# Layer 0 and the SSD norms re-cut: row sums in column groups, seven conv taps on VectorE, shift dots on TensorE, shift reads on SyncE's queue

## The chip, the cores and the metric

One core of a Trainium2 chip runs the whole kernel. The metric is the device time of one execution in microseconds (us), smaller is better. The kernel before took 1365.77 us in the median of 3 runs (1363.56 to 1369.64).

## The reference: what is computed

A trunk of two layers over x of 512 tokens by 1024 features in float32. Each layer is a mixer and a ConvFFN, each behind an RMSNorm that a condition vector c scales and shifts. The change touches layer 0's norm and mixer (a combined projection that feeds sliding-window attention and a Conformer convolution of 31 taps with a LayerNorm) and, in layer 1's Mamba-2 mixer, the `dt` projection and the four grouped norms.

```python
mod = silu(c) @ w_mod[i] + b_mod[i]
sh_m, sc_m, g_m, sh_f, sc_f, g_f = split(mod, 6)
h = rmsnorm(x, norm_mix[i]) * (1.0 + sc_m) + sh_m
...
def even_mixer(h, ...):
    q, k, v, conf_in = split(h @ w_in + b_in)
    merged = concat([swa_sink_attention(q, k, v, ...), conformer_conv(conf_in, ...)])
    return merged @ w_out

def conformer_conv(u, conv_w, conv_b, ln_g, ln_b):
    a, g = split(u, 2)
    h = causal_dwconv(a * sigmoid(g), conv_w, conv_b)      # 31 taps, 512 channels
    mu, var = mean(h), mean(square(h - mu))                # over the 512 channels
    return silu((h - mu) * rsqrt(var + LN_EPS) * ln_g + ln_b)
...
y = yg * rsqrt(mean(yg * yg, axis=-1) + NORM_EPS)          # ssd_mixer, 4 groups of 512 features
```

## The kernel before

**Layout.** Activations lie with 128 features on the partitions and 512 tokens in the free dimension. A weight is split in two rounded parts (`wh`, `wl`), an activation likewise (`hn` holds such pairs), and one product of 128 by 128 weights is three matmuls of 512 columns (`mm3`, lines 365 to 367). A product of 128 output features over 1024 inputs is thus 24 matmuls. Weights come in tiles `raw` of 512 KB on SyncE's (SP's) queue (line 304), ScalarE (ACT) rounds them to `wh` (line 312) and VectorE (DVE) makes `wl` (line 317).

**Order of the work.** Each mixer is a list of tasks with an engine, a cost, predecessors, and buffers taken and given back. `Plan.run` simulates the engines with those costs and, whenever one is free, emits its ready task of highest rank: the length of the path behind it plus a weight for its label from a table of numbers (`MIXER0`, `MIXER1`). Each engine and each DMA queue then runs its instructions in the order in which they were emitted.

**Layer 0's norm.** x comes in 8 tiles; ACT squares each (line 672); line 679 sums a square over its features with four matmuls of one column (the square is the weight, ones the moving column), 32 matmuls in all; ACT takes the root (699); `rstd_newton` (lines 405 to 409) refines it on DVE in five small instructions of 4 columns; `spread` (line 399) turns the columns into a row on all partitions. Then per feature tile: DVE computes the scale and the shift of the condition as a dot of 1024 columns each (`mod_dot`, line 571), `normed`, `upper` and `lower` (741, 745, 749) make the pair `hn`, and the first six outputs of the projection accumulate as `hn` appears (line 753). Line 651 issues idle matmuls (fillers) at three places of the norm.

**Convolution.** 512 channels are four chunks. A chunk's gated input (line 869) is stored to DRAM (872) and read back by `conv_fetch` (886) as four tiles `s`, one per 32 channels, each holding four shifted copies of these channels; stores and reads are issued on GpSimd's (POOL's) queue. `conv_product` (893) adds the taps in steps: a step is four matmuls of 512 columns, one for each group of 32 output channels, which covers four taps; eight steps (`CQ`) make 31 taps. Weights of these matmuls are diagonal blocks built by DVE (877); ACT adds the bias (898). The LayerNorm's mean is four matmuls with ones (1119), its squares' sums are 16 one-column matmuls (1110), then root, `rstd_newton` and `spread` as above.

**Layer 1.** `dt_in` is 24 matmuls with weights of 32 columns, `dt_tokens` four transposes; each of the four scan groups ends with the sums of `sz` (line 391, 4 matmuls), a root (1607), `rstd_newton` and `spread` before its rows can enter the output product.

Of the kernel before, what the change touches and what calls it, by code (L numbers as in the profile page):

```python
# [16 lines left out]
F32 = mybir.dt.float32  # L17
# [7 lines left out]
P = 128  # L25
# [9 lines left out]
CTAPS, CQ = 4, 8  # L35
# [4 lines left out]
_VEC = [("bmod", 96), ("nmix", 16), ("nffn", 16), ("fnorm", 8), ("bin", 14), ("ccw", 128), ("eye", 32),  # L40
# [29 lines left out]
WARM = (2, 2, 3)  # L70
# [152 lines left out]
def trunk(ctx: ExitStack, tc: tile.TileContext, xT_d, vecs_d, rows_d, dsk_d, pos_d, const_d, wss_d, wg0_d,  # L223
# [178 lines left out]

    def rstd_newton(ss, sd, width, e=0, n=NCH):
        v, y, a, y2 = (small(n) for _ in range(4))
# [216 lines left out]
    def even_layer(lp, cp, dp0):  # L621
# [26 lines left out]
        def warm(n):  # L648

            for _ in range(n):  # L650
                mm(g0[NG0 - 1][:, 0:2 * P], lhsT=ident, rhs=con[:, :2 * P], start=True, stop=True)
# [58 lines left out]
        rb_ = add("x_row", "PE", 2.1, x_row, [t], dict(ps=1))  # L710
# [54 lines left out]
        for kt in range(KT):  # L765
# [8 lines left out]
            s_ = add("h_dot", "DVE", 1.3, lambda kt=kt: mod_dot(st["ss", kt, 1], modv[:, 0, kt:kt + 1]), [ss_, *cbs], None, dict(mr=1))  # L774
            s_ = add("h_bias", "ACT", 0.29, lambda kt=kt: shift(kt), [s_, vl_])
# [1112 lines left out]
```

## Time and profile before

| what | value |
|---|---|
| median of 3 runs | 1365.77 us |
| profiled execution, time of its own | 1364.35 us |
| its span in the trace | 1362.5 us |
| mean granted TensorE clock | 0.986 |
| TensorE (PE) busy | 1335.4 us, 98% |
| VectorE (DVE) busy | 852.4 us, 63% |
| ScalarE (ACT) busy | 590.5 us, 43% |

The span is the time from the first to the last instruction that the profiler recorded; 1.85 us of the execution lie outside of it. Durations and sums below come from this one execution. [...]

### The profile page before, as it was taken

To read this page: it belongs to the slowest core of one execution; us is meant where nothing else is said; L and a number is where in the kernel's file an instruction comes from. 1 tells how busy PE (TensorE), PEld (TensorE's weight loads), DVE (VectorE), ACT (ScalarE), POOL (GpSimd) and SP (SyncE) were. 2 spreads that over 40 slices of the span, in tenths; PEclk is the share of its full clock that TensorE was granted. 3 is DMA by queue.
4 is the path that set the end of the run, shared out by engine and by line. 5 is a ranking of instruction groups with operands and counts; after the bars stand their busy time and mean duration, and the time that the engine had idled before them with its cause. 6 is when DMAs were issued, how large, how long until landed. Compare 5 with 4: busy or idle time off the path is not lost.

```text
span 1362.5 us, 17553 instructions
## 1 busy us (share of the span) xinstructions
PE 1335.4 (98%) x6878; PEld 1093.9 (80%) x6879; DVE 852.4 (63%) x1316; ACT 590.5 (43%) x938; POOL 95.7 (7%) x173
## 2 busy tenths in 40 slices
PE   8979999999999999999999999999999999999997
PEld 7726778988888888898887887878898888888886
DVE  5912898786576567667588684788665434444443
ACT  4512763543233223246686762765354313322333
POOL 5420110000000000010010100110000000000001
PEclk7989999999999999999999999999999999999998
DMA  9595453475565565322552432432223233223311
GB/s 333 194 191 129 138 194 118 140 232 172 183 210 168 183 214 191 105 89 67 153 169 79 156 93 80 139 126 79 76 78 111 90 100 107 92 89 108 100 55 63
DMA packets 58212, 183.71 MB, mean 135 GB/s; under 512 B 10064, under 2 KB 13200, under 8 KB 58128
## 3 DMA queue, kind: packets, MB, share of 16 engines
q1 hardware_dynamic: 45184, 152.24, 35.2%
q0 software_dynamic: 12256, 29.69, 7.5%
q8 instruction: 54, 0.88, 0.3%
q10 hardware_dynamic: 688, 0.66, 0.2%
q14 instruction: 30, 0.25, 0.1%
HBM read 179.26 MB, written 3.28 MB: 134 GB/s over the span
## 4 chain that ended last, share of the span: by engine, by line
PE 87%; DMA 4%; DVE 3%; issue 2%; ACT 2%; POOL 1%; DVEq 0%; ACTq 0%; POOLq 0%
PE ps L365 26%; PE ps L367 26%; PE ps L366 26%; DMA s<-uc 2%; PE ps L893 2%; DMA M<-scr 2%; PE ps L399 1%; PE ps L391 1%; PE ps L1573 1%; PE ps L679 1%; ACT M L1523 1%; PE ps L1565 1%; PE ps L1551 1%; DVE mr L571 1%; PE ps L1041 0%
## 5 line engine op out<-in xcount | busy, mean ns | idle before, releaser
L365 PE MATMUL ps<-hn,wh 128*128 128x512 f32 (+1 forms) x1214 | 460.1, 379 | 0.8 <-ACT hn L441 0.8
L366 PE MATMUL ps<-hn,wh 128*128 128x512 f32 (+1 forms) x1214 | 454.1, 374 | 0.4
L367 PE MATMUL ps<-hn,wl 128*128 128x512 f32 (+1 forms) x1214 | 454.0, 374 | 0.0
L317 DVE TENSOR_TENSOR wl<-raw,wh 128x1024 fp32r<-128x1024 f32 (+1 forms) x208 | 250.8, 1209 | 144.4 <-ACT wh L312 143.4
L312 ACT CAST wh<-raw 128x1024 fp32r<-128x1024 f32 (+1 forms) x208 | 213.1, 1028 | 219.2 <-PE ps L366 209.9
L365 PEld LDWEIGHTS ps<-hn,wh 128*128 128x128 f32 x1214 | 228.6, 188 | 43.0 <-issue 1.7
L366 PEld LDWEIGHTS ps<-hn,wh 128*128 128x128 f32 x1214 | 228.7, 188 | 42.0 <-issue 1.4
L367 PEld LDWEIGHTS ps<-hn,wl 128*128 128x128 f32 x1214 | 228.5, 188 | 41.0
L454 DVE SCALAR_TENSOR_TENSOR x<-ps,modv,x 128x512 f32<-128x512 f32 (+1 forms) x108 | 73.7, 689 | 119.6 <-PE ps L367 119.4
L365 PE MATMUL ps<-fh,wh 128*128 128x512 f32 (+1 forms) x380 | 142.2, 374 | 0.0
L366 PE MATMUL ps<-fl,wh 128*128 128x512 f32 (+1 forms) x380 | 141.9, 373 | 0.0
L367 PE MATMUL ps<-fh,wl 128*128 128x512 f32 (+1 forms) x380 | 141.9, 373 | 0.0
L571 DVE SCALAR_TENSOR_TENSOR mr<-mr,cb 128x1024 f32<-128x1024 f32 x96 | 116.1, 1218 | 3.5 <-DMA mr<-in_wss_dram 2.2
L1281 ACT ACTIVATE tmp<-ps,vecs 128x512 f32<-128x512 f32 x44 | 34.3, 780 | 115.4 <-PE ps L367 115.4
L1282 DVE SCALAR_TENSOR_TENSOR tmp<-ps,vecs,tmp 128x511 f32<-128x511 f32 x44 | 32.9, 748 | 80.0 <-ACT tmp L1281 80.0
L366 PEld LDWEIGHTS ps<-fl,wh 128*128 128x128 f32 x380 | 71.5, 188 | 12.8
L365 PEld LDWEIGHTS ps<-fh,wh 128*128 128x128 f32 x380 | 71.5, 188 | 12.6
L367 PEld LDWEIGHTS ps<-fh,wl 128*128 128x128 f32 x380 | 71.5, 188 | 12.6
L429 POOL TENSOR_TENSOR ssq<-ssq,tmp 128x512 f32<-128x512 f32 x10 | 13.4, 1338 | 805.1 <-ACT tmp L428 805.1
L290 ACT CAST fh<-tmp 128x512 fp32r<-128x512 f32 x44 | 27.3, 620 | 96.4 <-DVE tmp L1286 96.4
L1284 ACT ACTIVATE tmp<-tmp 128x512 f32<-128x512 f32 x44 | 27.8, 633 | 74.9 <-DVE tmp L1283 74.9
L291 DVE TENSOR_TENSOR fl<-tmp,fh 128x512 fp32r<-128x512 f32 x44 | 30.5, 693 | 30.2 <-ACT fh L290 30.2
(277 smaller groups left out, 1500.0 us busy)
## 6 DMA issues: line engine op xcount, KB each, us to landing
raw<-in_w_dram SPq DMA_DIRECT2D x176, 512.0 KB, 3.7
mr<-in_wmod_dram SPq DMA_DIRECT2D x56, 512.0 KB, 3.6
raw<-in_w_dram SPq DMA_DIRECT2D x32, 448.0 KB, 3.3
mr<-in_wmod_dram POOLq DMA_DIRECT2D x24, 512.0 KB, 5.1
mr<-in_wss_dram SPq DMA_DIRECT2D x16, 512.0 KB, 6.2
M<-scr POOLq DMA_DIRECT2D x16, 512.0 KB, 4.7
s<-uc POOLq DMA_DIRECT2D x16, 270.0 KB, 15.1
raw<-in_wg_dram SPq DMA_DIRECT2D x8, 384.0 KB, 5.7
```

What stands on the lines that cost most here:

```text
L290: nc.scalar.copy(h, src)
L291: (eng or nc.vector).tensor_tensor(l, src, h.bitcast(F32), ALU.subtract)
L312: nc.scalar.copy(h, self.raw[i].rearrange("p (k m) -> p k m", m=P))
L317: eng.tensor_tensor(l, self.raw[i].rearrange("p (k m) -> p k m", m=P), h.bitcast(F32), ALU.subtract)
L365: mm(ps, lhsT=w[0], rhs=ah, start=first, stop=False)
L366: mm(ps, lhsT=w[0], rhs=al, start=False, stop=False)
L367: mm(ps, lhsT=w[1], rhs=ah, start=False, stop=last)
L454: stt(x[:, m, hs], ps, gate(m), x[:, m, hs], ALU.mult, ALU.add)
L571: stt(raw, raw, 1.0, mod_pool[2], ALU.mult, ALU.mult, accum_out=out)
L1281: act(c, pg, AF.Identity, bias=vec("fcb", i), scale=vec("fcw", 3 * i + 2))
L1282: stt(c[:, 1:], pg[:, :T - 1], vec("fcw", 3 * i + 1), c[:, 1:], ALU.mult, ALU.add)
L1284: act(c, c, AF.Silu)
```

## The change

- **Row sums** (`row_sums`, `row_spread`): ones are the weights, the squares move. Four matmuls of 128 columns, one per chunk of 128 tokens, run in the four column groups of the array and leave the sums with the 128 tokens along the free dimension; `row_spread` copies them to all partitions. Used for the LayerNorm's mean (16 matmuls and 4, in place of 4 of 512 columns) and variance, and for the four scan groups. Root and `rstd_newton` then work on 128 columns in place of 4. In layer 0's first norm DVE adds six of the eight squares (`x_add`, 5 instructions), and 12 of the 32 one-column matmuls stay.
- **Taps**: `CQ` is 6; taps 24 to 30 are done on ACT (`late0`, 4 instructions, bias included) and DVE (`late`, 24 instructions), and DVE adds the two parts (`csum`, 4).
- **Shift dots**: of the 16 condition dots of the first norm, 4 go from DVE to PE (`pe_dot`: 8 matmuls of 128 columns in four column groups; ACT copies the result, one small matmul adds the groups).
- **Fillers**: 16 idle matmuls of 128 columns as tasks of their own, in place of 7 of 256 at fixed places.
- **Queues**: the 16 shift reads are issued on SP's queue (532 columns in place of 540); the stores stay on POOL's.
- **dt**: the high and low weights stand side by side in 64 columns: 16 matmuls in place of 24, and four plain matmuls in place of the transposes.
- **Order**: both tables of weights are new.

```diff
-CTAPS, CQ = 4, 8
+CTAPS, CQ = 4, 6
+NLATE = 31 - CTAPS * CQ
...
-WARM = (2, 2, 3)
+WARM = 16
+PE_DOTS = 4
...
-MIXER1 = {'xdt': 122, 'differ': 108, ...}
+MIXER1 = {'xdt': 58, 'differ': -6, ...}
-MIXER0 = {'sigmoid': 15, 'square': -70, ...}
+MIXER0 = {'sigmoid': 13, 'square': -70, ..., 'late': 40, 'late0': 139, 'csum': 91, 'warm': -14, ...}
...
+    def row_sums(ps, src, first, last):
+        for c in range(NCH):
+            mm(ps[32 * c:32 * c + 32, :], lhsT=ones.broadcast_to([P, 32]), rhs=src[:, c * P:(c + 1) * P],
+               start=first, stop=last, tile_position=(0, 32 * c))
+
+    def row_spread(rows_):
+        ps = bank()
+        for c in range(NCH):
+            mm(ps[:, c * P:(c + 1) * P], lhsT=ident[:, 32 * c:32 * c + 1].broadcast_to([P, P]), rhs=rows_,
+               start=True, stop=True)
+        return ps
...
+        def x_add(k):
+            tt(st["xq", 0], st["xq", 0], st["xq", k], ALU.add)
...
+        def pe_dot(kt):
+            o = st["pd", kt] = bank((P, 2 * P))
+            for n in range(0, KT, 4):
+                for g in range(4):
+                    k = n + g
+                    mm(o[32 * g:32 * g + 32, 0:P], lhsT=cond[:, k:k + 1].broadcast_to([P, 32]),
+                       rhs=st["ss", kt, 1][:, k * P:(k + 1) * P], start=(n == 0), stop=(n > 0), tile_position=(0, 32 * g))
...
-                nc.gpsimd.dma_start(u4[g], bass.AP(src.tensor, src.offset + 32 * g * CROW,
+                nc.sync.dma_start(u4[g], bass.AP(src.tensor, src.offset + 32 * g * CROW,
...
-        def conv_bias(i):
+        def late_first(i):
             cv[i] = tile_s()
-            act(cv[i], st["co", i], AF.Identity, bias=vec("ccb", i))
+            act(cv[i], us[i], AF.Identity, bias=vec("ccb", i), scale=vec("cct", NLATE * i + NLATE - 1))
+
+        def late_tap(i, d):
+            stt(cv[i][:, d:], us[i][:, :T - d], vec("cct", NLATE * i + NLATE - 1 - d), cv[i][:, d:], ALU.mult, ALU.add)
+
+        def conv_sum(i):
+            tt(cv[i], st["co", i], cv[i], ALU.add)
...
-            mm(st["mb"], lhsT=ones.broadcast_to([P, P]), rhs=cv[i], start=(i == 0), stop=(i == 3))
+        def mean_in():
+            st["mr"] = row_tile()
+            act(st["mr"], st["mu"], AF.Copy, scale=-1.0 / 512.0)
...
-                mm3(st["dtf"][0:32, :], (dwh[:, kt, :], dwl[:, kt, :]), *hn[kt], kt == 0, kt == KT - 1)
+                if kt:
+                    mm(o[0:32, :], lhsT=dw[:, kt, 0:32], rhs=hn[kt][1], start=False, stop=False)
+                mm(o[0:64, :], lhsT=dw[:, kt, :], rhs=hn[kt][0], start=(kt == 0), stop=(kt == KT - 1))
```

**PE at the end of the first norm.** Before, every square has its four one-column matmuls (`ps_212<-ones,tmp`), and the last of them stand ahead of the row's spread (`ps_299`) and of the first product:

```order
L679 MATMUL ps_212<-ones,tmp_193 128x1 [waits DVE_49,Activation_49]
L679 MATMUL ps_212<-ones,tmp_196 128x1 [waits Activation_49]
...
L679 MATMUL ps_212<-ones,tmp_232 128x1 [waits Activation_49]
L679 MATMUL ps_212<-ones,tmp_238 128x1 [waits Activation_49]
L651 MATMUL ps_180<-con 128x256 x2
L399 MATMUL ps_299<-con,sm_292 128x128 [waits DVE_49]
L651 MATMUL ps_180<-con 128x256 x3
L753 MATMUL ps_175<-hn_322,wh_268 128x512 [waits Activation_49]
```

Now (line 700 is the old 679, 404 the old 399, 797 the old 753):

```order
L700 MATMUL ps_243<-ones,tmp_193 128x1 [waits DVE_49]
L670 MATMUL ps_180<-con 128x128
L700 MATMUL ps_243<-ones,tmp_228 128x1 [waits Activation_49]
L773 MATMUL ps_260<-mr_223,con 32x128 [waits DMAHW3_49]
L700 MATMUL ps_243<-ones,tmp_232 128x1 [waits Activation_49]
L781 MATMUL ps_260<-vecs,tmp_273 128x1 [waits DMAHW1_49,Activation_49]
L670 MATMUL ps_180<-con 128x128 x5
L404 MATMUL ps_305<-con,sm_296 128x128 [waits DVE_49]
L773 MATMUL ps_313<-mr_253,con 32x128 [waits DMAHW6_49]
L670 MATMUL ps_180<-con 128x128 x2
L797 MATMUL ps_175<-hn_332,wh_275 128x512 [waits Activation_49]
```

The sum of six squares and the last two squares are left, a shift dot that waits for its load stands ahead of the last of them, and a second dot follows the spread.

**PE around the convolution.** Before, the last rows of the product ahead of it, the first step of its first chunk and the later places of the mean (line 1119):

```order
L367 MATMUL ps_714<-hn_590,wl_631 128x512
L893 MATMUL ps_754<-s_704,mr_712 32x512 [waits DMASW4_49,DVE_49,Activation_49]
...
L893 MATMUL ps_806<-s_743,mr_692 32x512 [waits DMASW0_49,Activation_49]
...
L893 MATMUL ps_851<-s_839,mr_698 32x512 [waits DMASW5_49]
...
L1119 MATMUL ps_894<-s_847,ones 128x512 [waits Activation_49]
L893 MATMUL ps_898<-s_884,mr_794 32x512 [waits DMASW1_49,DVE_49]
...
L1119 MATMUL ps_894<-s_892,ones 128x512 [waits Activation_49]
L365 MATMUL ps_934<-hn_322,wh_701 128x512
...
L1119 MATMUL ps_894<-s_896,ones 128x512 [waits Activation_49]
```

Now (line 944 is the old 893; `s_798` to `s_801` are the second chunk's tiles, `s_752` to `s_755` the first's, `s_955` to `s_958` the last's; 412 is `row_sums`):

```order
L372 MATMUL ps_808<-hn_625,wl_663 128x512
L944 MATMUL ps_844<-s_798,mr_834 32x512 [waits DMAHW0_49,DVE_49,Activation_49]
...
L944 MATMUL ps_885<-s_752,mr_874 32x512 [waits DMAHW4_49,DVE_49]
...
L944 MATMUL ps_929<-s_910,mr_871 32x512 [waits DMAHW4_49,Activation_49]
...
L412 MATMUL ps_977<-s_731,ones 32x128 [waits DVE_49]
L370 MATMUL ps_983<-hn_332,wh_747 128x512 [waits Activation_49]
...
L412 MATMUL ps_977<-s_735,ones 32x128 x4
L944 MATMUL ps_1017<-s_955,mr_879 32x512 [waits DMAHW1_49,Activation_49]
...
L412 MATMUL ps_977<-s_738,ones 32x128 [waits DVE_49]
...
L412 MATMUL ps_977<-s_881,ones 32x128 [waits DVE_49]
...
L419 MATMUL ps_1088<-rw_1086,con 128x128 [waits Activation_49]
```

One product more stands ahead of the convolution (90 `mm3` matmuls in place of 66), the second chunk goes first, and a product stands between the third chunk and the last.

**SP's queue.** Before, weight tiles follow each other with no shift read among them:

```order
L304 DMA raw_609<-in_w_dram 128x1024 [waits DMAHW0_49,DVE_49]
L304 DMA raw_643<-in_w_dram 128x1024 [waits DMAHW6_49,DMAHW1_49,DVE_49]
L304 DMA raw_655<-in_w_dram 128x1024 [waits DMAHW7_49,DMAHW2_49,DVE_49]
L304 DMA raw_741<-in_w_dram 128x1024 [waits DMAHW3_49,DMAHW0_49,DVE_49]
L304 DMA raw_752<-in_w_dram 128x1024 [waits DMAHW2_49,DVE_49]
```

Now the reads of three chunks (`s<-uc`) stand ahead of the seventh weight tile, and a part of the last chunk's ahead of the eighth; they wait for the stores, and everything behind them on this queue waits with them:

```order
L309 DMA raw_687<-in_w_dram 128x1024 [waits DMAHW7_49,DMAHW2_49,DVE_49]
L309 DMA raw_724<-in_w_dram 128x1024 [waits DMAHW3_49,DMAHW0_49,DVE_49]
L937 DMA s_752<-uc_108 128x1x532 [waits DMAHW4_49,DMASW1_49]
...
L937 DMA s_798<-uc_109 128x1x532 [waits DMASW3_49,DMASW2_49]
...
L937 DMA s_910<-uc_110 128x1x532 [waits DMAHW4_49,DMASW5_49,DMASW3_49]
...
L309 DMA raw_922<-in_w_dram 128x1024 [waits DMAHW0_49,DVE_49,Activation_49]
L937 DMA s_955<-uc_111 128x1x532 [waits DMASW7_49,DMASW4_49,DMAHW1_49,PE_49,Pool_49]
L309 DMA raw_926<-in_w_dram 128x1024 [waits DMAHW2_49,DVE_49,Activation_49]
L937 DMA s_956<-uc_111 128x1x532 [waits DMAHW3_49,PE_49,Pool_49]
```

On POOL's queue the reads are gone; the four stores follow each other, and loads for the later condition dots come behind them.

## Rows read from the trace of the kernel before

**Rows 1.** The page: PE's busy time (part 1), the chain by engine (part 4).
```profile
PE 1335.4 (98%) x6878; PEld 1093.9 (80%) x6879; DVE 852.4 (63%) x1316; ACT 590.5 (43%) x938; POOL 95.7 (7%) x173
...
PE 87%; DMA 4%; DVE 3%; issue 2%; ACT 2%; POOL 1%; DVEq 0%; ACTq 0%; POOLq 0%
```

**Rows 2.** Windows: length, busy PE PEld DVE ACT POOL, clock, DMA share, GB/s.
```profile
11.50:20.50 9.00, 9.00 (x43) 9.00 (x44) 3.45 (x5) 2.53 (x5) 7.53 (x20) 0.50 1.03 410
25.70:57.00 31.30, 30.50 (x136) 24.23 (x135) 31.06 (x57) 16.89 (x31) 8.96 (x16) 1.00 0.63 217
...
72.05:117.30 45.25, 37.33 (x260) 12.88 (x259) 4.33 (x4) 4.84 (x6) 8.77 (x14) 0.89 0.93 203
131.10:198.20 67.10, 65.28 (x476) 49.91 (x475) 60.39 (x129) 49.16 (x123) 7.88 (x15) 0.97 0.42 138
```

**Rows 3.** The chain of waits from 0 to 30 us: start, us, what.
```profile
9.09 11.35 PE ps L679 x64
...
22.36 1.72 PE ps L399 x8
```

**Rows 4.** Timelines of ACT (one row), then DVE (two), 2 to 36 us: start, us, what.
```profile
10.86 0.63 ACT L672 ACTIVATE tmp<-x 128x512 f32<-128x512 f32 x1 [0.26 <-PE ps L679]
...
13.37 1.29 DVE L571 SCALAR_TENSOR_TENSOR mr<-mr,cb 128x1024 f32<-128x1024 f32 x1 [2.19 <-DMA mr<-in_wss_dram]
...
24.19 0.75 DVE L741 SCALAR_TENSOR_TENSOR tmp<-x,modv,ps 128x512 f32<-128x512 f32 x1 [0.28 <-PE ps L399]
```

**Rows 5.** The chain of waits from 56 to 135 us: start, us, what.
```profile
69.58 25.09 DMA s<-uc
...
94.70 13.92 PE ps L893 x122
108.62 1.05 PE ps L1119 x2
109.68 7.63 PE ps L893 x64
...
118.37 0.23 PE ps L365
...
123.85 0.86 PE ps L1119 x2
```

**Rows 6.** PE's waits from 57 to 118 us: us in total, times, longest.
```profile
PE ps L893 <- DMA s<-uc: 7.9, 5, 2.7
```

**Rows 7.** Windows within the shifts' time, columns as in the second group.
```profile
75.00:95.00 20.00, 13.20 (x71) 2.82 (x74) 2.45 (x2) 2.78 (x3) 2.23 (x4) 0.74 1.04 218
65.00:70.00 5.00, 5.00 (x24) 4.14 (x23) 4.56 (x5) 0.00 (x0) 5.00 (x8) 1.00 0.39 96
```

**Rows 8.** The stores of line 872: microseconds from issue to landing.
```profile
DMA to landing us min/median/max: 3.0/3.0/22.1
```

**Rows 9.** PE's groups by line and shape: xcount | busy us, mean ns | idle before.
```profile
L893 PE MATMUL ps<-s,mr 128*32 128x512 f32 x256 | 36.4, 642 | 7.9 <-DMA s<-uc 7.9
...
L1110 PE MATMUL ps<-ones,tmp 128*128 128x1 f32 x32 | 4.0, 246 | 0.0
L391 PE MATMUL ps<-ones,sz 128*128 128x1 f32 x32 | 3.9, 242 | 1.0 <-DVE sz L1600 1.0
...
L365 PE MATMUL ps<-hn,tmp 128*32 128x512 f32 x8 | 3.2, 395 | 0.0
```

**Rows 10.** DVE's groups by line and shape, columns as in the ninth group.
```profile
L1282 DVE SCALAR_TENSOR_TENSOR tmp<-ps,vecs,tmp 128x511 f32<-128x511 f32 x44 | 32.9, 748 | 80.0 <-ACT tmp L1281 80.0
...
L1415 DVE TENSOR_TENSOR acs<-acs,eacs 128x128 f32<-128x128 f32 x8 | 2.3, 289 | 0.2
...
L406 DVE RECIPROCAL sm<-sm 128x4 f32<-128x4 f32 x6 | 1.0, 166 | 0.0
...
L1408 DVE RECIPROCAL dtd<-dtd 128x128 f32<-128x128 f32 x1 | 1.0, 952 | 0.0
```

**Rows 11.** ACT's table loads before a norm's root, columns as in the ninth group.
```profile
L1607 ACT ACT_TABLE_LOAD x4 | 5.1, 1283 | 0.1
```

More of the change, by code (lines that the diff above doesn't have):

```diff
@@ L248, in small, with row_tile @@
         return sp.tile([P, n], dt, tag="sm", name=nm("sm"), bufs=24)
+    def row_tile():
+        return sp.tile([P, P], F32, tag="rw", name=nm("rw"), bufs=5)
     def hn_tile(which):
@@ L401, in spread @@
         return ps
+    def row_sums(ps, src, first, last):
[8 more added lines that the diff above has]
+        return ps
     def rstd_newton(ss, sd, width, e=0, n=NCH):
-        v, y, a, y2 = (small(n) for _ in range(4))
+        v, y, a, y2 = (small(n) if n < P else row_tile() for _ in range(4))
         ts(v, ss, 1.0 / width, (1e-6, 1e-5)[e], ALU.mult, ALU.add)
@@ L646, in even_layer, with warm @@
         add = plan.add
-        def warm(n):
-            for _ in range(n):
-                mm(g0[NG0 - 1][:, 0:2 * P], lhsT=ident, rhs=con[:, :2 * P], start=True, stop=True)
+        def warm():
+            mm(g0[NG0 - 1][:, 0:P], lhsT=ident, rhs=con[:, :P], start=True, stop=True)
         plan.group = "norm"
@@ L905, in conv_tasks @@
             b_ = plan.add("gated", "DVE", 0.69, lambda: gated(i, pa), [a_], None, dict(ps=2, tmp=1))
-            d_ = plan.add("taps", "DVE", 1.3, lambda: conv_taps(i), [a_], dict(mr=1))
-            c_ = plan.add("store", "SIDE", 1.0, lambda: conv_store(i), [b_])
-            c_ = plan.add("shifts", "SIDE", 3.6, lambda: conv_fetch(i), [c_, margins_], dict(u4=1))
-            c_ = plan.add("conv", "PE", 7.4, lambda: conv_product(i), [c_, d_], dict(ps=1), dict(mr=1, u4=1))
-            conv_done[i] = plan.add("cbias", "ACT", 0.69, lambda: conv_bias(i), [c_], None, dict(ps=1))
+            d_ = plan.add("taps", "DVE", 0.95, lambda: conv_taps(i), [a_], dict(mr=1))
+            e_ = plan.add("late0", "ACT", 0.69, lambda: late_first(i), [b_])
+            for d in range(1, NLATE):
+                e_ = plan.add("late", "DVE", 0.69, lambda d=d: late_tap(i, d), [e_])
+            c_ = plan.add("store", "SIDE", 1.5, lambda: conv_store(i), [b_])
+            c_ = plan.add("shifts", "DMA", 3.6, lambda: conv_fetch(i), [c_, margins_], dict(u4=1))
+            c_ = plan.add("conv", "PE", 1.0 * CQ, lambda: conv_product(i), [c_, d_], dict(ps=1), dict(mr=1, u4=1))
+            conv_done[i] = plan.add("csum", "DVE", 0.69, lambda: conv_sum(i), [c_, e_], None, dict(ps=1))
         for i in range(3):
@@ L1718, in group @@
             st["m_last"], st["s_last"] = weighs, s_ins
-            t = plan.add("sums", "PE", 0.86, sc.sums, sq[3:], dict(ps=1), dict(sz=4))
-            t = plan.add("root", "ACT", 0.2, sc.root, [t], table="sqrt")
-            t = plan.add("newton", "DVE", 0.8, sc.newton, [t], None, dict(ps=1))
+            t = plan.add("sums", "PE", 0.3, sc.sums, sq[3:], dict(ps=1), dict(sz=4))
+            t = plan.add("root", "ACT", 0.35, sc.root, [t], table="sqrt")
+            t = plan.add("newton", "DVE", 2.1, sc.newton, [t], None, dict(ps=1))
             rb = plan.add("rows", "PE", 1.0, sc.rows, [t], dict(ps=1))
```

102 lines of the change are left out of this document (60 added, 42 removed).

## The prediction

> **What bounds the kernel now.** I read the page first: PE is busy in 98% of the span and has 87% of the chain [rows 1], so whatever does not shorten PE's work or its waits is worth nothing. But a busy PE is not always a fast one. So I cut the span into stages with the windows and looked for a low granted clock, and for PE's busy time below the window's length [rows 2]. Three places of layer 0 stand out; the rest of the span, both ConvFFNs among it, the change leaves alone except for layer 1's mixer.
>
> The first is the norm at the start. [...] ACT had its last square at 10.86 + 0.63 = 11.49 us; the row arrives for the first `normed` at 24.19 [rows 4]. [...]
>
> The second is the convolution, 45.25 us of which PE is busy 37.33, at a mean clock of 0.89 [rows 2]. The chain shows what it waits for: a shift read that takes 25.09 us, until 94.66; then 122 records of line 893 in 13.92 us without a gap [rows 5]. A step of four matmuls is 8 records, so a step costs 8 x 13.92 / 122 = 0.91 us when the data are there. PE's waits name the same reads, 7.9 us in five waits [rows 6].
>
> The third is the attention, 67.10 us with PE busy 65.28 and DVE 60.39, or 90% [rows 2]: DVE is close to being the bound there.
>
> **The change part by part.** I sum against the profiled execution's 1364.35 us, 1.4 below the median of the runs, which is nothing beside the terms.
>
> *Start.* Eight squares make eight rounds of sums, 11.35 / 8 = 1.42 us each [rows 3]; three rounds stay. DVE's five additions, at most 0.75 each [rows 10], follow the squares as they come. The last round stands behind the first shift dot, whose load lands at 13.37 [rows 4]. The dot is eight matmuls of 128 columns in four groups: a quarter of two steps, 0.46 us, or 0.9 at half clock. So the sums end at 13.37 + 0.9 + 1.42 = 15.7; the time from there to `normed` was 24.19 - 20.44 = 3.75 [rows 3, 4], which gives 19.4, a gain of 4.8. On PE two dots and four small matmuls then stand among the first products, which fill PE (30.50 of 31.30 [rows 2]): + 0.8. **Start: -4.0.** Ends: -1 (loads or DVE, which is busy 31.06 of that window, hold the products back) and -6.
>
> *Conv work.* Eight of 32 steps go: **-7.3.** The 24 late taps, 24 x 0.75 = 18 us of DVE [rows 10], lie beside it: DVE is busy 4.33 of the 45.25 us [rows 2]. Without that cover they would be in the way of the LayerNorm; that is the second rival.
>
> *Conv wait.* 45.25 - 32 x 0.91 - 2 x 1.05 (the two means inside [rows 5]) = 13.9 us are waits and half clock. Before, twelve reads need from about 64.8, when the last of three stores has let the first be issued, to 94.66, 2.5 us each. Now they leave from SP's queue ahead of the weight loads, while PE does one product more (24 x 0.23 = 5.5 us [rows 5]) before it wants them. With only shift reads running, the DMA engines were 0.39 busy at 96 GB/s; with weight loads beside them, 1.04 at 218 GB/s [rows 7]. Both rows say about 210 to 250 GB/s for engines that are kept busy, or 1.1 to 1.3 us for a read of 270 KB. From a first read at about 60 us, the second chunk's (eighth read) are there at 70, the third's at 75; PE wants them at 73 and 84. **All 13.9 go.** The other end is the old pace (first rival), 8 back.
>
> [...]
>
> *Mean.* Before 2 x 1.05 + 2 x 0.86 = 3.8 [rows 5]; now four sums of a quarter step, 0.23 each, and a spread of 1.72 / 2 = 0.86 (its row was at half clock [rows 3]): 1.8. **-2.0.** *Variance:* 4.0 [rows 9] becomes 4 x 0.23: **-3.1.** *Scan sums:* 3.9 [rows 9] likewise: **-3.0.** Ends for the three together: -5 (if PE, modelled busy in these rows, was not all lost) and -8.1.
>
> [...] The trace shows no price where PE goes from 893 (32-column groups) to 1119 (the whole array) and back: 94.70 + 13.92 = 108.62, + 1.05 = 109.67, and the next begins at 109.68 [rows 5]. [...]
>
> *Attention.* The LayerNorm's chain grows by a `csum`, 0.75, and by a longer Newton: five instructions of 0.17 [rows 10] become one reciprocal of 0.95 and four of at most 0.29, 2.1 in place of 0.83, + 1.3. PE has products to do meanwhile, but DVE is 90% full. I charge the chain's growth once: **+2.0.** Ends: -1.8 (the stage's PE idle time goes) and +7 (below).
>
> *Layer 1.* Eight matmuls of `dt` go, 8 x 0.23: **-1.8.** Four Newtons grow by 1.3 each, and ACT gets three table loads more, of 1.28 [rows 11]. They lie under the 24 matmuls between a group's sums and its rows, 5.5 us. I charge one Newton: **+1.3**; ends 0 and 4 x 1.3 + 3 x 1.28 = +9.
>
> *Sum.* -4.0 - 7.3 - 13.9 - 2.0 - 3.1 - 3.0 + 2.0 - 1.8 + 1.3 = -31.8, so 1332.5.
>
> **The rivals.**
>
> 1. *The reads keep their old pace*, 2.5 us each, since the packets set it and not the queue. From 60 us the eighth lands at 80, 7 us after PE wants it, and the last chunk's about 1 us late. For it: the engines are full at 75 to 95 us [rows 7]. Against: only when weight loads run too. 1340.5.
>
> 2. *DVE bounds the attention stage.* Late taps, `csum` and the longer Newton add 18 + 3 + 1.3 = 22 us of DVE; some 15 fit beside the shorter convolution, 7 come out behind it. For it: 90% [rows 2]. Against: the idle DVE of the convolution is far more than 18 us now. The sum without the +2.0, plus 7: 1337.5.
>
> [...]
>
> 4. *The start gains nothing*: the products come earlier but at half clock or without data, as the fillers do not hold the clock: 1336.5. For it: the 0.50 of that stretch [rows 2], where PE was never idle and yet slow.
>
> 5. *Slower*: SP's queue is blocked. It waits in order, and weight tiles now stand behind the last chunk's reads, which wait for its store. One store took 22.1 us where the others took 3.0 [rows 8]. If this store lands so late, the weight loads behind it come as late, and PE, with three products' weights in hand (16.5 us), runs dry; what is behind must then be fetched at the pace at which it is used. To be slower than before it has to cost over 31.8 us, so it decides only from a store that lands some 50 us after its issue. Against it: the late store stood behind twelve reads on POOL's queue, which are gone from there. With 45 us lost: 1377.5.
>
> **How the numbers follow.** Forecast 0.57; rival 1: 0.14; rival 2: 0.13; rival 4: 0.08; rival 3: 0.04; rival 5: 0.04. The good ends together (start -6, attention -1.8, layer 1 0) lie 2 + 3.8 + 1.3 = 7.1 below the forecast, 1325.4; PE's idle of 1.0 before the scan sums [rows 9], its 0.8 in the window of the first products and the attention's clock of 0.97 (67.10 x 0.03 = 2.0) [rows 2] may go as well, which makes 1321.6; the range begins at 1321. It ends at 1347, with rivals 1 and 2 together (1345.5) and rival 3. A measurement of this kernel can tell about 0.5%, or 6.8 us, from no change. All cases but the fifth are over 0.5% faster; a little is left for several bad ends at once: faster 0.95, same 0.02, slower 0.03.
>
> **What would show it.** The chain should show about 35 records of sums less at the start and the first product at about 20.5 us; line 893's successor 192 records in about 22 us, with waits for shift reads under 1 us; the attention's window shorter or equal, DVE over 90% in it; no idle PE of over 2 us in layer 1's mixer. [...] The prediction is wrong if the time is above 1347 or below 1321.

## The result and the profile after

The changed kernel takes 1377.1 us in the median of 4 runs (1375.4 to 1379.8), the kernel before 1365.5 beside it: ratio 1.0075, 95% interval 1.0049 to 1.0101. It is **slower by 0.75%**, where 1332.5 was forecast and a slower kernel had been given a chance of 0.03. Its profiled execution spans 1373.7 us, 11.2 more than before.

The page of the changed kernel, busy time and chain, to be read beside [rows 1]:

```profile
PE 1327.8 (97%) x6889; PEld 1083.4 (79%) x6893; DVE 875.0 (64%) x1341; ACT 594.7 (43%) x946; POOL 84.9 (6%) x157
...
PE 82%; issue 9%; DVE 3%; DMA 3%; ACT 2%; POOL 1%; POOLq 0%; DVEq 0%; ACTq 0%
```

PE has 7.6 us less to do and needs 11.2 us more: its share of the chain fell from 87% to 82%. So work went, and waits came. The windows by stage (columns as in [rows 2], the granted clock as a share of full speed; the third is the convolution with its means and one product, the fourth the attention):

```profile
11.50:20.50 9.00, 7.36 (x48) 6.93 (x49) 4.62 (x12) 3.00 (x8) 7.65 (x20) 0.63 1.03 410
25.60:57.35 31.75, 31.75 (x170) 25.58 (x171) 29.13 (x52) 17.95 (x35) 9.25 (x19) 1.00 0.66 222
77.90:135.80 57.90, 41.13 (x241) 12.52 (x240) 19.89 (x27) 5.23 (x6) 3.23 (x6) 0.79 0.53 163
135.80:207.00 71.20, 66.90 (x497) 50.39 (x501) 59.53 (x124) 48.71 (x124) 8.07 (x15) 0.95 0.39 131
```

The start is at half clock for most of the window (0.63 in the mean, where it was 0.50). In the convolution PE is busy 41.13 of 57.90 us and the clock has fallen to 0.79. PE's waits (us in total, times, longest):

```profile
PE ps L944 <- DMA s<-uc: 16.8, 8, 4.8
...
PE ps L1084 <- ACT s L1064: 3.4, 2, 3.0
PE ps L1637 <- DVE M L1594: 3.4, 3, 1.8
```

The wait for shift reads grew from 7.9 us [rows 6] to 16.8; line 944 is the old 893. PE's timeline at its beginning (start, us, what, in brackets the idle time before it and what ended it):

```profile
82.68 1.88 PE L944 MATMUL ps<-s,mr 128*32 128x512 f32 x2 [4.77 <-DMA s<-uc]
86.09 1.92 PE L944 MATMUL ps<-s,mr 128*32 128x512 f32 x2 [1.52 <-DMA s<-uc]
92.47 1.92 PE L944 MATMUL ps<-s,mr 128*32 128x512 f32 x2 [4.46 <-DMA s<-uc]
95.06 12.51 PE L944 MATMUL ps<-s,mr 128*32 128x512 f32 x96 [0.68 <-DMA s<-uc]
```

PE has done its products at 77.9 and then gets one shift tile of the second chunk after the other, at 82.7, 86.1, 92.5 and 95.1. Two records of one tile are done, in 1.88 to 1.92 us, then it waits for the next; the granted clock is 0.51 from 82 to 90 us and 0.50 from 90 to 95. The first read was issued at 65.8; the eighth, the last of the second chunk's, is used at 95.1: 3.7 us each. SP itself is held up when it issues them (ns, least, median, most; then the first and the last start):

```profile
L937 SPq DMA_DIRECT2D s<-uc x16: 511/1868/6503, 65.8 to 107.5; - x16
```

Between 82 and 90 us the fourth store and two loads for condition dots are on the way beside the reads (DMA share 0.70 at 211 GB/s). The windows in which little else moves:

```profile
70.00:75.00 5.00, 5.00 (x23) 4.14 (x23) 5.00 (x10) 0.00 (x0) 0.00 (x0) 1.00 0.26 98
75.00:80.00 5.00, 2.91 (x13) 2.06 (x11) 4.97 (x8) 0.69 (x1) 0.00 (x0) 1.00 0.26 101
...
90.00:95.00 5.00, 1.92 (x2) 0.18 (x2) 0.00 (x0) 0.00 (x0) 0.00 (x0) 0.50 0.26 101
```

The experiments below start from this reading: **the DMA share stands at 0.26, at 98 to 101 GB/s.** Of 16 engines that is 4.2 at a time in the mean (an estimate, 0.26 x 16). With all engines busy, at a share of 1.03, the start of the same kernel moved 410 GB/s, of which a quarter is 102. At 98 to 101 GB/s a read of 266 KB takes 2.7 us (an estimate); the rest of the 3.7 I put down to the time until the first one moves and to the other transfers from 82 to 90 us; it was not measured by parts.

### The profile page after: what moved, and what is told of

Same layout as the page of the kernel before. It is cut to its first block, busy times and chain, and to the rows that moved or that the text cites. A ratio compares the mean times of both kernels' runs of the same rounds, so it can differ in the third digit from the quotient of the medians.

```text
span 1373.7 us, 17643 instructions
## 1 busy us (share of the span) xinstructions
PE 1327.8 (97%) x6889; PEld 1083.4 (79%) x6893; DVE 875.0 (64%) x1341; ACT 594.7 (43%) x946; POOL 84.9 (6%) x157
## 4 chain that ended last, share of the span: by engine, by line
PE 82%; issue 9%; DVE 3%; DMA 3%; ACT 2%; POOL 1%; POOLq 0%; DVEq 0%; ACTq 0%
PE ps L370 25%; PE ps L371 25%; PE ps L372 25%; PE ps L797 2%; DMA M<-scr 1%; PE ps L1637 1%; DVE s L953 1%; DMA mr<-in_wmod_dram 1%; PE ps L1615 1%; POOL mr L583 1%; PE ps L404 1%; PE ps L396 1%; PE ps L1603 1%; PE ps L1629 0%; ACT M L1587 0%
## 5 line engine op out<-in xcount | busy, mean ns | idle before, releaser
L591 DVE SCALAR_TENSOR_TENSOR mr<-mr,cb 128x1024 f32<-128x1024 f32 x92 | 111.2, 1219 | 3.9 <-DMA mr<-in_wmod_dram 3.8
L944 PE MATMUL ps<-s,mr 128*32 128x512 f32 x192 | 34.9, 720 | 16.8 <-DMA s<-uc 16.8
```

The source lines that it names most:

```text
L591: stt(raw, raw, 1.0, mod_pool[2], ALU.mult, ALU.mult, accum_out=out)
L944: mm(o[32 * g:32 * g + 32, :], lhsT=st["cw", i][:, g, n, :], rhs=st["u4", i][g][:, 4 * n:4 * n + T], start=(n == 0), stop=(n == CQ - 1), t ...
```

## The experiments

Times are medians; each ratio is to the kernel before on the same chip, where its median lay between 1365.5 and 1368.1 us. The places in the table are from the traces: PE's first product, the last record of the convolution, and three of the sums of squares of line 391, now 396: the first ones, at the end of the attention; those of layer 1's norm; the last ones, at the end of layer 1's ConvFFN.

| kernel | us | ratio, 95% interval | first product | conv end | first such sum | layer 1's norm | last sum | span |
|---|---|---|---|---|---|---|---|---|
| before | 1365.5 | | 25.7 | 116.7 | 232.9 | 598.7 | 1350.8 | 1362.5 |
| after | 1377.1 | 1.0075 (1.0049 to 1.0101) | 25.6 | 135.1 | 242.0 | 607.9 | 1359.5 | 1373.7 |
| reads_pool | 1354.7 | 0.9910 (0.9878 to 0.9941) | 25.6 | 111.7 | 221.1 | 587.0 | 1340.8 | 1352.1 |
| reads_by_channel | 1345.0 | 0.9839 (0.9807 to 0.9872) | 25.5 | 104.2 | 212.5 | 578.4 | 1330.1 | 1343.7 |
| before_reads_sp | 1385.5 | 1.0134 (1.0101 to 1.0168) | 25.7 | 136.1 | 252.3 | 618.2 | 1369.7 | 1383.8 |
| before_by_channel_sp | 1354.7 | 0.9912 (0.9883 to 0.9941) | 25.7 | 103.2 | 219.5 | 585.3 | 1339.2 | 1352.8 |
| before_by_channel_pool | 1353.0 | 0.9903 (0.9878 to 0.9928) | 26.1 | 101.4 | 217.6 | 583.5 | 1335.4 | 1350.3 |
| by_channel_seven_steps | 1361.8 | 0.9966 (0.9949 to 0.9982) | 24.1 | 103.6 | 226.0 | 591.8 | 1345.4 | 1359.0 |
| by_channel_old_order1 | 1354.0 | 0.9906 (0.9881 to 0.9932) | 23.4 | 102.2 | 211.1 | 576.9 | 1338.2 | 1351.9 |
| by_channel_no_pe_dots | 1352.5 | 0.9895 (0.9873 to 0.9916) | 23.3 | 100.2 | 216.3 | 582.2 | 1337.7 | 1351.3 |
| narrow_newton | 1345.6 | 0.9848 (0.9823 to 0.9872) | 23.2 | 101.9 | 211.3 | 577.2 | 1328.8 | 1342.9 |
| fewer_late_taps | 1346.4 | 0.9848 (0.9821 to 0.9874) | | | | | | |
| no_fillers | 1345.2 | 0.9833 (0.9808 to 0.9857) | 24.7 | 103.4 | 208.8 | 574.6 | 1325.8 | 1339.5 |
| old_scan | 1343.8 | 0.9828 (0.9805 to 0.9852) | 23.9 | 102.6 | 209.0 | 574.9 | 1325.7 | 1339.3 |
| old_scan_no_fillers | 1345.9 | 0.9854 (0.9821 to 0.9887) | 24.4 | 105.2 | 210.7 | 576.6 | 1328.8 | 1342.5 |
| fewer_condition_loads | 1342.9 | 0.9826 (0.9799 to 0.9853) | 23.7 | 102.4 | 206.7 | 572.5 | 1327.3 | 1339.6 |
| ln_later | 1355.1 | 0.9905 (0.9884 to 0.9925) | 23.3 | 101.6 | 216.1 | 585.2 | 1339.2 | 1352.9 |
| ln_between | 1344.6 | 0.9834 (0.9815 to 0.9853) | 25.5 | 104.0 | 211.4 | 577.7 | 1330.0 | 1343.6 |

### The reads: queue, shape or contention

*reads_pool*, the changed kernel:

```diff
-                nc.sync.dma_start(u4[g], bass.AP(src.tensor, src.offset + 32 * g * CROW,
+                nc.gpsimd.dma_start(u4[g], bass.AP(src.tensor, src.offset + 32 * g * CROW,
```

> The changed kernel with one edit: the 16 shift reads are issued on POOL's queue again. In the changed kernel PE waits for them and runs at half clock for about 27.6 us in the convolution. [...] Theory C (contention with the weight loads sets the pace, the queue does not matter): no change, 1377 within 5.

1354.7: contention (theory C) is out, the queue matters by 22 us. Where the DMA share was 0.26 on SP's queue, from 75 to 80 us, it is 0.96 now:

```profile
75.00:80.00 5.00, 2.92 (x14) 2.11 (x13) 4.97 (x8) 0.69 (x1) 0.00 (x0) 1.00 0.96 140
```

PE waits once for a read, 1.6 us until 82.60, and then goes on without a wait, so that the eighth read is there by about 84.6, 2.3 us each from the first issue at 66.2 (an estimate, two pairs of records of 1.02 us behind 82.60), where it was 3.7.

*reads_by_channel*, reads still on SP's queue. A shift tile has 128 partitions, 4 shifts of 32 channels; now the channels are the outer dimension, and the diagonal weights (`ccw`, and an `eyc` of its own) are laid out likewise:

```diff
-                                                       [[1, CTAPS], [CROW, 32], [1, CWIN]]))
+                                                       [[CROW, 32], [1, CTAPS], [1, CWIN]]))
...
-        "ccw": cw[:CTAPS * CQ].reshape(CQ, CTAPS, 4, 4, 32).transpose(1, 4, 2, 3, 0).reshape(P, 16 * CQ),
+        "ccw": cw[:CTAPS * CQ].reshape(CQ, CTAPS, 4, 4, 32).transpose(4, 1, 2, 3, 0).reshape(P, 16 * CQ),
```

> The changed kernel, reads still on SP's queue, but the read's outer dimension is the 32 channels and the inner one the 4 shifts (the diagonal weights are laid out to match). Theory A (the outer dimension 4 limits a read to 4 engines): the DMA share while reads run is near 1, a read takes 1.1 to 1.5 us, PE waits under 2 us for them, about 1350 us. Theory B (SP's queue is slow for such reads in itself) and theory C (contention): as the changed kernel, 1377 within 5, with a DMA share of 0.26 when only reads run.

1345.0, by 32 us faster than the changed kernel, with the same bytes on the same queue. Its windows in the reads' time, in the convolution and in the attention:

```profile
70.00:75.00 5.00, 5.00 (x24) 4.14 (x23) 5.00 (x9) 0.00 (x0) 0.00 (x0) 1.00 0.94 307
77.70:105.00 27.30, 27.30 (x242) 11.25 (x242) 19.92 (x27) 5.24 (x6) 3.22 (x6) 1.00 0.72 263
105.00:175.00 70.00, 65.69 (x497) 49.42 (x498) 58.39 (x121) 48.50 (x123) 7.53 (x14) 0.95 0.40 130
```

The DMA share is 0.94 at 307 GB/s where it was 0.26 at 98, and PE is busy for all of the 27.30 us that took 57.90. Its convolution in the timeline of PE, its reads from issue to landing (us; least, median, most), and their issues on SP (as above):

```profile
77.74 15.66 PE L944 MATMUL ps<-s,mr 128*32 128x512 f32 x144
...
99.47 5.33 PE L944 MATMUL ps<-s,mr 128*32 128x512 f32 x48
```

```profile
DMA to landing us min/median/max: 3.5/5.1/8.9
```

```profile
L937 SPq DMA_DIRECT2D s<-uc x16: 513/590/923, 65.8 to 87.4; - x16
```

*before_reads_sp* and *before_by_channel_sp*, the same two edits in the kernel before, the first `nc.gpsimd` to `nc.sync` alone, the second with the channels outermost as well:

> The kernel before with one edit: the 16 shift reads on SP's queue. Theories A and B: a read takes 3.6 us in place of 2.5, the DMA share is 0.26 while only reads run, PE waits 12 to 18 us longer: about 1380 us. Theory C: no change, 1365.5 within 5.

> The kernel before with the reads on SP's queue and their outer dimension the 32 channels. Theory A: the reads land before PE wants them or nearly so, 10 to 14 us of wait and half clock go, about 1353 us. Theories B and C: as the kernel before with its reads on SP's queue, 1365 to 1380.

1385.5 and 1354.7. PE's waits for the reads, 7.9 us in the kernel before, are, in the first and in the second:

```profile
PE ps L893 <- DMA s<-uc: 19.8, 9, 5.1
```

```profile
PE ps L893 <- DMA s<-uc: 0.8, 1, 0.8
```

*before_by_channel_pool* closes the square, the shape changed and the queue not:

> The kernel before, reads on POOL's queue as they were, only their outer dimension is the 32 channels. Theory A (the number of DMA engines that a read uses is all): as the same reads on SP's queue, 1354.7 within 3. If POOL's queue itself costs these reads time as well, several microseconds above that, 1358 to 1365.

1353.0, the same as on SP's queue within what can be told. So with 4 shifts outermost the queue is worth 20 us (1385.5 against 1365.5), and with 32 channels outermost nothing (1354.7 against 1353.0). Theory A holds for SP's queue as far as the share of busy engines goes: there it was 0.26 with reads of the old shape, and the shape alone lifts it to 0.94. On POOL's queue it was 0.96 with the old shape (above), at 140 GB/s. How many engines a single read had, and which, no row shows for either queue. Other sizes of the outermost dimension, 8 or 16, were not run.

### What else kept the forecast from being met

With the reads mended 12.5 us are left to the forecast. The next runs start from *reads_by_channel*.

*by_channel_seven_steps*, `CQ` 7 in place of 6:

> The changed kernel with reads by channel on SP's queue (1345.0) and seven steps of the convolution on PE in place of six, three taps on ACT and DVE in place of seven: PE gets 4 steps, 3.65 us; DVE loses 16 of 28 late-tap instructions on ACT and DVE, 12 to 16 x 0.66 = 8 to 10 us. In the attention, from the end of the convolution to the first sums of the output's squares, that kernel takes 5.65 us longer than the kernel before does. Theory D (DVE has too much to do there, the second rival): 3 to 5.6 of these come back, 1343 to 1345.5. Theory O (the order and length of the chains, not the amount of DVE work): 1348.7.

1361.8, a miss for both theories. Fewer tasks in the list gave another order for all of layer 0: from the end of the convolution to the first sum it takes 122.4 us, against 108.3. Two of PE's waits that the other kernel does not have at this length:

```profile
PE ps L370 <- DVE x L474: 7.6, 1, 7.6
...
PE ps L1102 <- ACT s L1091: 3.5, 1, 3.5
```

The run says nothing on the taps; it points to what a table of weights is worth after the list that it was made for has changed. *by_channel_no_pe_dots*, `PE_DOTS` 0, suffers from the same:

> The changed kernel with reads by channel on SP's queue and no shift dots on PE: all 16 dots on DVE. Theory S1 (in the start PE is the late one: sums, dots and fillers run one after the other at half clock, and a dot stands ahead of the last sum): the first product comes 1 to 2 us earlier, but DVE gets 4.9 us while it makes the first products' inputs; 1344 to 1346. Theory S2 (DVE was the bound of the first products, the dots on PE are worth their 4.9 us): 1348 to 1350.

1352.5, above both expectations. The first product does come 2.2 us earlier, as S1 says, but so it does in other runs whose start has nothing changed (23.2 in *narrow_newton*), and what follows is in another order. Undecided.

So the next three keep the list and its costs, and leave out only what is emitted. *fewer_late_taps*:

```diff
         def late_tap(i, d):
+            if d > 2:
+                return
```

> The changed kernel with reads by channel on SP's queue, same order; four of the six late taps of DVE in each chunk are left out (these taps are not computed): 16 instructions, 10.6 us of DVE less beside the convolution. Theory D (the added DVE work runs over into the attention, the second rival): 3 to 5.6 us faster, 1339.5 to 1342. Theory O (the attention waits for chains in an unlucky order while DVE's added work is covered): 1345 within 1.

1346.4, the median of four executions (1344.2 to 1348.5). A fifth, the profiled one, took 4660.1 us and is left aside, and its trace with it. 10.6 us of DVE are worth nothing that can be told: theory D, the second rival of the prediction, falls as far as the taps are concerned.

*narrow_newton* and *no_fillers*:

```diff
-                self.col = rstd_newton(self.ss, self.sd, 512.0, 0, P)
+                c = rstd_newton(self.ss[:, 0:4], self.sd[:, 0:4], 512.0, 0, 4)
+                nc.vector.tensor_copy(self.sd[:, 0:4], c)
+                self.col = self.sd
...
-            mm(g0[NG0 - 1][:, 0:P], lhsT=ident, rhs=con[:, :P], start=True, stop=True)
+            pass
```

> The changed kernel with reads by channel on SP's queue (1345.0), same order; in the four scan groups the Newton step works on 4 of the 128 columns only (the other columns keep the plain root, so these norms are not computed), which takes some 1.1 us of DVE from each of the four chains from sums to rows. Theory N (the longer chains of root, Newton and row give back what the shorter sums save in layer 1): 2 to 4 us faster, the waits for M shrink from 3.2. Rival (these chains lie under other work): 1345 within 1.

> The changed kernel with reads by channel on SP's queue, same order, the 16 fillers left out. In its trace the spread of the first norm's row stands behind five fillers that run at half clock: the Newton step ends at 20.6 and the spread begins at 22.2. Theory F (fillers only lie in the way): 1 to 2 us faster, about 1343.5. Rival (without them PE stays at half clock longer when the products begin): 0 to 3 us slower.

1345.6 and 1345.2: both nothing that can be told. The longer Newton of the scan groups is covered, and what fillers may help or hurt is too little to be seen.

*by_channel_old_order1* puts the old `MIXER1` back, *old_scan* the old sums, root, Newton and rows as well, and the old cost of `dt`, so that layer 1's order is that of before:

> The changed kernel with reads by channel on SP's queue and layer 1's mixer in its old table of weights. From layer 1's norm to the end the changed kernel is only 0.4 us shorter than the kernel before, where the terms said 3.5; PE waits 3.2 us for the decayed matrices M, 0.5 before. Theory: the new order makes these waits; they go, about 1342.5. Rival: they come from the longer Newton and the three table loads and stay, 1345 within 1.

> The changed kernel with reads by channel on SP's queue, the scan groups' sums, root, Newton and row, and layer 1's order, as before; only dt stays new. Layer 1's norm to the end took 752.1 us before and 751.7 now. Theory N (the new sums win nothing in the end): 1344 within 1.5, dt's 1.8 us at most gained. If the new sums were worth their 3.0 us: 1346.5 to 1348.

1354.0 and 1343.8; the first missed both of its expectations. From layer 1's norm to the last sum it is 761.3 us with new sums in the old order, 751.7 with new sums in the new order, 750.8 with old sums in the old order, and 752.1 in the kernel before. The new sums, which take PE 1.7 us in place of 3.9, win nothing; the new table does no more than repair what they cost in the old order, 9 us. PE's waits in this stretch are 9.6 us there and 3.9 with the new table; the other 3.7 us stand in its busy time (751.2 against 747.5 us) and are not explained. The longest waits are for DVE, at three kinds of places:

```profile
PE ps L1637 <- DVE M L1594: 3.9, 2, 3.0
...
PE ps L419 <- DVE rw L429: 1.9, 1, 1.9
...
PE ps L1629 <- DVE st L1623: 1.4, 1, 1.4
```

and with all of layer 1 old only the attention's wait and a short one for the squares are left among these:

```profile
PE ps L1084 <- ACT s L1064: 3.4, 2, 3.0
...
PE ps L396 <- DVE sz L1664: 1.3, 1, 1.3
```

*fewer_condition_loads* leaves 16 of the 24 loads and dots of the attention stage out, *ln_later* and *ln_between* change the weight of `ln` in `MIXER0` from 150 to -60 and to 0:

> The changed kernel with reads by channel on SP's queue (1345.0), same order; 16 of the 24 loads and dots of the next condition vectors in the attention are left out (the ConvFFN's scale and shift are not computed, a constant stands in). Theory G (in the attention each load on POOL's queue waits for a buffer that a dot on DVE frees, the dots wait for the loads, and the residuals at the end wait for DVE behind them: a chain of loads and dots sets the end): most of the 5.65 us that the attention is too long come back, 1339 to 1341. Rival (the chains of softmax set it, PE's 3.0 us wait for the exponentials): 1344 within 1.5.

> The changed kernel with reads by channel on SP's queue (1345.0), one weight of layer 0's table changed: the LayerNorm's scaling, and with it its four SiLUs, comes after the softmax exponentials of all heads, not ahead of those of the last two. Theory P (PE's 3.0 and 0.4 us of waits for the exponentials, and the half clock after them, come from the LayerNorm standing ahead on ACT and DVE): these waits go, 2 to 5 us faster, 1340 to 1343. Rival (the LayerNorm is needed as early as it comes, for the output projection): as much wait appears ahead of the projection, 1345 within 1.5 or slower.

> As the other, with a weight between: one of the four SiLUs stays ahead of the last exponentials, three come behind them, at the price of one more table load on ACT, 1.28 us. Theory P: 1 to 4 us faster than 1345.0. Rival: 1345 within 1.5 or slower.

1342.9, 1355.1 and 1344.6. Without the loads the way from the convolution's end to the first sum takes 104.3 us in place of 108.3. But single executions differ here: four traces with the same layer 0 (*reads_by_channel*, *by_channel_old_order1*, *narrow_newton*, *old_scan*) lie between 106.4 and 109.4. The whole kernel is 2.1 us shorter, and the intervals overlap; PE's 3.0 us wait for the exponentials stays. With the LayerNorm later that wait goes and others come, 10 us in the three longest, of which 1.9 us, for `x`, stood there before:

```profile
PE ps L419 <- DVE rw L429: 4.1, 1, 4.1
PE ps L370 <- DVE x L474: 3.5, 2, 3.1
...
PE ps L396 <- DVE ssq L499: 2.6, 1, 2.6
```

So neither explains the attention alone; its cause stays open. *old_scan_no_fillers*, the two best edits together:

> The changed kernel with reads by channel on SP's queue, scan groups and layer 1's order as before, and no fillers: the candidate for the fastest. If both edits are worth what their single runs showed against 1345.0 (-1.2 and +0.2, each within about 2): 1344 within 1.5.

1345.9. The fastest version that computes everything is *old_scan* with 1343.8 (ratio 0.9828), with *reads_by_channel*, *ln_between*, *no_fillers* and *old_scan_no_fillers* not to be told from it; all beat both kernels.

## Why the prediction was wrong, point by point

**The step that failed** is the conv wait, "All 13.9 go". It rested on 1.1 to 1.3 us for a read, taken from 96 GB/s at a share of 0.39 and 218 GB/s at 1.04 [rows 7] as "engines that are kept busy". On SP's queue, where the change put the reads, they did not keep the engines busy: the share was 0.26, a read took 2.7 us by the rate alone, and the eighth was used 3.7 us a read after the first issue. I took the 0.39 for room; it was measured in the first 5 us after the first issue on the other queue and says nothing of SP's. With 32 channels outermost the price was high enough: at 307 GB/s a read takes 0.9 us (an estimate), and PE does the 144 records of three chunks from 77.74 on without a wait for one. (The first read was issued at 65.8 and not at about 60; once reads are fast this costs nothing, since PE is free at 77.7.)

The old pace was misread as well, and with it the first rival. The read that lands at 94.66 [rows 5] is the eighth and not the twelfth, as POOL issues eight of them in a row, the last at 69.58. POOL and PE of the kernel before:

```profile
64.80 5.45 POOL L886 DMA_DIRECT2D s<-uc  x8 [1.21 <-DMA uc<-s]
```

```profile
72.05 1.05 PE L893 MATMUL ps<-s,mr 128*32 128x512 f32 x2
...
91.34 1.04 PE L893 MATMUL ps<-s,mr 128*32 128x512 f32 x2 [0.62 <-DMA s<-uc]
```

So the first eight took 3.7 us each there too, beside weight tiles, and the twelfth landed at 101.1. The kernel before takes the first chunk first and works on it from 72.05 on; the changed one takes the second chunk first and cannot go far before the eighth read. At 3.7 us a read the rival's sum gives 89.6 in place of 80 for the eighth, and about 1350 in place of 1340.5 (an estimate), beyond the range. What was missing altogether is a price for the edit from below: I bounded a move between queues by the old queue's pace alone.

In us: where four products, the convolution and its sums for the mean are done (three of the four sums in the changed kernels, whose last one follows later), the kernel before is at 131.05 and the changed one at 135.8, 4.8 later. Yet 7.3 of work and 3.1 of the mean (3.8 less three sums of 0.23) are gone, and the stage began 0.35 later: so the term was 4.8 + 7.3 + 3.1 - 0.35, about +15 in place of -13.9. With reads by channel the point is at 105.0.

**The first rival's ground**, that the queue does not set the pace of the reads, held with 32 outermost (1354.7 and 1353.0 us) and not with 4: there the queue was worth 20 us (1385.5 against 1365.5), and on SP's the DMA share was 0.26, so that three quarters of the engines' time was idle.

**The convolution's other terms** held. 131.05 - 105.02 = 26.0 us is gained once the reads are fast, 0.25 of it in the start. Work, wait and mean up to there were priced at 7.3 + 13.9 + 3.1 = 24.3, so together they gave somewhat more.

**The start**, -4.0 forecast, gave 0.15: first product at 25.59 against 25.74. That is what rival 4 said. In other traces with the same start the first product comes at 23.2 to 25.6 us, in the four traces with the old start at 25.7 to 26.1; so the gain is 0.1 to 2.6 us, and this trace is among the poor ones. I let the sums end at 15.7; they end at 19.35. DVE and PE of the changed kernel:

```profile
9.26 3.82 DVE L694 TENSOR_TENSOR tmp<-tmp,tmp 128x512 f32<-128x512 f32 x4
...
20.35 0.25 DVE L429 SCALAR_TENSOR_TENSOR sm<-sm,sm 128x4 f32<-128x4 f32 x1
```

```profile
13.14 1.27 PE L700 MATMUL ps<-ones,tmp 128*128 128x1 f32 x8 [1.82 <-DVE tmp L694]
...
14.83 1.71 PE L700 MATMUL ps<-ones,tmp 128*128 128x1 f32 x8
16.47 1.08 PE L773 MATMUL ps<-mr,con 128*32 128x128 f32 x16
17.48 1.87 PE L700 MATMUL ps<-ones,tmp 128*128 128x1 f32 x8
...
19.63 2.48 PE L670 MATMUL ps<-con 128*128 128x128 f32 x10
21.91 1.92 PE L404 MATMUL ps<-con,sm 128*128 128x128 f32 x8
...
25.59 0.72 PE L797 MATMUL ps<-hn,wh 128*128 128x512 f32 x2 [0.24 <-ACT hn L789]
```

DVE's four last additions take 3.82 us, between 0.69 and 1.17 us each, and end at 13.1, 2.2 us after the last square; why two of them are longer is not settled. Then sums, filler, dot and sums run one behind the other, each round 1.3 to 1.9 us, from 14.5 us on at a granted clock of 0.50; I had counted one round behind the dot only. And the spread waits behind five fillers: Newton ends at 20.60, the spread begins at 21.91. Without fillers the spread begins at 20.5 and the first product at 24.7 (*no_fillers*), and the time of the kernel stays the same within what can be told.

**Attention and variance**, +2.0 - 3.1, gave +4.4: from 131.05 to 232.9 before, from 135.8 to 242.0 now, 5.6 with reads by channel. Some 1.4 us of it belong to the mean: its fourth sum (0.35 us of the chain with reads by channel) and its spread (1.09) now stand behind that point. Of the rest one place is seen, a wait for the exponentials, with a granted clock of 0.50 from 185 to 189 us behind it; the kernel before has such waits of 1.6 us in all, the longest 1.0.

```profile
185.04 0.48 PE L1084 MATMUL ps<-con,s 128*128 128x128 f32 x1 [3.01 <-ACT s L1064]
185.95 1.35 PE L1084 MATMUL ps<-con,s 128*128 128x128 f32 x5 [0.43 <-ACT s L1064]
```

The cause is not settled: fewer taps, fewer condition loads and two other places of the LayerNorm gave the whole kernel 2 us at most, and `csum` and the LayerNorm's own longer Newton were not tested by themselves.

**Layer 1**, -3.0 - 1.8 + 1.3, gave -0.5: PE's saving came back as waits for DVE (3.4 us for `M`, 0.5 before). It is not the longer Newton (*narrow_newton*); with old sums and old order the layer is as fast. What makes `M` late was not tested.

**The rest** of the 11.2 us: the middle is equal (365.8 us before and 365.9 now between the first such sum and layer 1's norm), and the last stores land 2.5 us later after the last sum (14.2 against 11.7 us); the other traces show from 11.3 to 14.9 there, with the same code.

Rival 3 stands in the chances and in the upper end of the range for a price of each change of the matmuls' shape; no run shows such a term. With reads by channel a sum in four column groups takes 0.35 us of the chain between two groups of score matmuls of other shapes, against the 0.23 counted, so 0.1 us for two changes at most. Rival 5 named the right place, SP's queue, but the wrong cause: no store was late (6.8 us at most). That its 1377.5 lies beside the measured 1377.1 is chance, as its 45 us were picked and not worked out.

## What to carry to other kernels

Before a transfer is moved to another queue, look at the DMA share in a stretch where only its kind is on the way, on the queue where it will be. A share of 0.26 at a steady 98 to 101 GB/s meant here that the reads left most of the engines' time unused, and then the outermost dimension of the access pattern counted, and not the bytes: with 32 in place of 4 the share was 0.94 at 307 GB/s. By this the kernel before gained 13 us on POOL's queue (1353.0 against 1365.5), 11 us together with the move to SP's (1354.7), and the changed kernel 32 us (1345.0 against 1377.1). To read a pace from a chain, count the transfers that have landed by then, and not those that are needed. And a table of priorities that was made for one list of tasks is part of the code: after any change of the list its old numbers, or a neighbour's, can cost more than the edit.

## What was not expected

- With reads of 266 KB and an outermost dimension of 4 the DMA share stood at 0.26 on SP's queue, at 98 to 101 GB/s, with no other load beside them from 70 to 80 us; with 32 outermost it was 0.94 at 307 GB/s from 70 to 75. The queue changes nothing then (1354.7 and 1353.0 us).
- The half clock at the start comes with fillers and, in one of two traces, without them: in *old_scan_no_fillers* the granted clock is 0.50 from 14 to 24 us, in *no_fillers* 1.00 from 8 to 34, and the last round of sums takes 1.87 us in both, as in the changed kernel. When it ends differs between executions: from 22 to 24 us it is 0.50 in the changed kernel, 0.69 in *reads_by_channel* and 1.00 in *by_channel_old_order1*, three kernels with the same start. In such kernels the first product stands anywhere from 23.2 to 25.6 us.
- New sums that take 2.2 us off PE cost 9 us in the order that was made for the old ones.
